# A ScalarE clock in the ordering model of a Trainium2 trunk kernel, and weight parts laid between a head's updates

## The chip, the core and the metric

The kernel runs on one core of a Trainium2 chip: TensorE (PE) multiplies, VectorE (DVE), ScalarE (ACT) and GpSimd (POOL) do the elementwise work, SyncE (SP) issues most transfers. Each engine takes its own instructions strictly in the order of the program and waits for others through semaphores. The metric is the device time of one execution in microseconds (us); less is better. The time before is the median of three runs.

## What is computed

A trunk of two layers on x of 1 x 1024 x 1024, all in float32. Layer 1 mixes tokens with a gated linear recurrence (8 heads of 128), layer 2 with attention in a window of 128; behind each stands a gated feed-forward part with a causal convolution of width 3. Every sublayer ends with a LayerNorm of ALPHA * h + sublayer. The change bears on the mixer of layer 1:

```python
def hgrn2_mixer(h, w_in, lower_bound, g_norm_w, w_out):
    q, f, i, g = jnp.split(h @ w_in, 4, axis=-1)
    ...
    fg = lb + (1.0 - lb) * jax.nn.sigmoid(heads(f))
    o = hgrn2_chunkwise(jax.nn.silu(heads(q)), 1.0 - fg, heads(i), jnp.log(fg))
    o = o * lax.rsqrt(jnp.mean(jnp.square(o), -1, keepdims=True) + RMS_EPS)
    o = o * g_norm_w * jax.nn.silu(heads(g))
    return o.reshape(B, S, D) @ w_out

# hgrn2_chunkwise, per head: S_t = diag(f_t) S_(t-1) + k_t v_t^T ;  o_t = S_t^T q_t
```

## The kernel before

A float32 product is made of three passes in a reduced format (`mm3`, L194 to L196): each operand is split into a high part, which ScalarE casts, and a low part, the rest, which VectorE subtracts (`low_part`, L169). L196 is the first pass that reads the low part of the weights.

The recurrence stage lies at some 24 to 545 us of the span. Its input products h @ w_in for heads 1 to 7 come in 14 units: unit 2(h-1) gives q and f of head h (kind "q"), the next one i and g (kind "v"). A unit is computed by a Strassen-Winograd scheme with seven products p1 to p7 of quarter matrices, each of 4 x 3 matmuls of 128x512, in the order 1, 5, 4 of the unit before, 6, 2, 3, 7. The weight side of a product is either a loaded quarter or a sum of quarters. `prepare` makes them: `cast` copies the high part on ScalarE (L1252, tile WR<-raw) and queues a job for the low part on VectorE (L169, WR<-raw,WR); sums of quarters are jobs too (L1260, raw<-raw,raw). WR has eight rows; `ROW` tells which product uses which. The four buffers raw0 to raw3 take the loaded quarters (L726, 512 KB each).

The results stand in four PSUM banks (psmm). `collect` has them read: ScalarE copies (L1320, L1334, L1388), VectorE additions (L1342, L1381, L1394) and gate functions (L1403, L1417, L1418, L1423).

Meanwhile the head before runs through `recur`: seven rounds of updates of qp, kp and tot on VectorE (`update`, L1095, L1097, L1100), scores on TensorE (L200, tile psax), masked placings of them on VectorE (`place`, L1038 and L1059), copies of halves on ScalarE (`stash`, L1082 and L1083) and of score blocks (L1076, L1154), transposes of the values (L204, VT to V, by L1388 and L1436), the products of values and keys (V,kd), a scan of the state St on VectorE (L1177, L1179), and the products V,A and St,qp that make the head's output.

The order in which all this is issued is set by `Order`, a small model that runs while the program is recorded. It carries a clock `t` for TensorE and `v` for VectorE; generators (`spawn`, `later`) are resumed when `t` reaches their due time, and between groups of matmuls `tick` lets them issue. Low parts and sums wait in the list `jobs`, first in, first out:

```python
def job(delay, us, make, key=None):
    jobs.append((od.t + delay, us, make, key))
def lay():
    if jobs and jobs[0][0] <= od.t:
        lay_job()
        return True
def need(key):
    while key not in done_jobs:
        lay_job()
```

`lay` is called as a filler when VectorE's clock is less than 1.5 us ahead; `product` calls `need`, which lays all jobs ahead of the one wanted. None of these times reach the chip; only the order does.

Ahead of the units, `sums_of` (L863) forms differences of quarters of the input on GpSimd, 12 subtractions of 128x512, read by ScalarE (L873) and VectorE (L874).

Of the kernel before, what the change touches and what calls it, by code (L numbers as in the profile page):

```python
# [54 lines left out]
class Order:  # L55
# [52 lines left out]
def trunk(ctx: ExitStack, tc: tile.TileContext, a: dict, out: bass.AP):  # L108
# [594 lines left out]
    with tc.tile_pool(name="t", bufs=1, reuse_waits="tile") as raws, hgrn_pool as hp:  # L703
# [29 lines left out]
        jobs, done_jobs = [], set()  # L733

        def job(delay, us, make, key=None):
            jobs.append((od.t + delay, us, make, key))

        def lay_job():
            ready, us, make, key = jobs.pop(0)
            make()  # L740
            od.vec(us)
            done_jobs.add(key)

        def lay():
            if jobs and jobs[0][0] <= od.t:
                lay_job()
                return True
            return False

        def need(key):  # L750
            while key not in done_jobs:
                lay_job()
# [107 lines left out]
        def sums_of(t):  # L860
            a11, a12, a21, a22 = [quarter(b, i) for b in (t, t + 4) for i in range(2)]
            for dst, x0, x1 in ((a11, a21, a11), (a21, a22, a21), (a22, a11, a22)):
                nc.gpsimd.tensor_tensor(dst, x0, x1, op=sub)  # L863

        def split_sum(t, which):
# [8 lines left out]
            job(0.9, 0.69, lambda: nc.vector.scalar_tensor_tensor(lo, src, scale, hi.bitcast(F32), op0=ALU.mult, op1=sub),  # L874
                ("x", which, t))

        with tc.tile_pool(name="ep", bufs=1, reuse_waits="tile") as ep:
# [33 lines left out]
            with tc.manual_schedule(engines={EN.PE, EN.SP, EN.Activation, EN.DVE}):  # L911
# [64 lines left out]
                for tp, after in ((2, 2), (1, 6)):  # L976
# [12 lines left out]
                for t in range(2, 4):  # L989
                    sums_of(t)  # L990
# [34 lines left out]
        def recur(h, qs, fg, kp):  # L1025
# [37 lines left out]
            def blocks(i, pv, K, Q):  # L1063
# [9 lines left out]
                def put():  # L1073
                    for b in range(P // (2 * m)):
                        o = 2 * m * b
                        nc.scalar.copy(A[o:o + m, :, o + m:o + 2 * m], pv[o:o + m, :, o + m:o + 2 * m])  # L1076
                return put

            def stash(i, t):
# [3 lines left out]
                nc.scalar.copy(halves(t)[:, :, 0, :], halves(kp)[:, :, 0, :])  # L1083
                return t
# [3 lines left out]
            def update(i):  # L1088
                m = 1 << i
                nb = S // (2 * m)  # L1090
                Tm, off = level
                qv = qp.rearrange("p (b u m) -> p b u m", u=2, m=m)
# [13 lines left out]
            nc.vector.tensor_tensor(r0, qs, kp, op=ALU.mult)  # L1106
            nc.vector.tensor_tensor(qp, qs, fg, op=ALU.mult)
            od.vec(4.4)
            r1 = hp.tile([P, S // 2], F32, name="r1")
            nc.vector.tensor_tensor(r1, kp[:, 0::2], qp[:, 1::2], op=ALU.mult)  # L1110
            update(0)
            gates_read[0] = h
            r2 = hp.tile([P, 2, S // 4, 2], F32, name="kd")
            for j in range(2):
                nc.vector.tensor_tensor(r2[:, j], kp[:, j::4].unsqueeze(2).to_broadcast([P, S // 4, 2]),
                                        qp.rearrange("p (b u) -> p b u", u=4)[:, :, 2:], op=ALU.mult)
            yield od.behind(-1.0, 5.0)
# [34 lines left out]
            for b in range(P // BL):  # L1152
                bs = slice(b * BL, (b + 1) * BL)
                nc.scalar.copy(A[bs, :, bs], Ab[bs])  # L1154
            yield wait
# [8 lines left out]
            nc.scalar.copy(kd, ps)  # L1164
            keys_done[0] = h
# [26 lines left out]
        def norm(h, pv):  # L1192
# [3 lines left out]
            for c in range(NB):  # L1196
                if c == NB // 2:
                    yield 2.4 if h < NH - 1 else 1.4
                nc.scalar.activation(junk, pv[:, c, :], AF.Square, accum_out=ss[:, c:c + 1])
            nc.gpsimd.tensor_scalar(ss, ss, 1.0 / P, RMS_EPS, op0=ALU.mult, op1=ALU.add)  # L1200
# [36 lines left out]
        last = len(units) - 1  # L1237
        raw_of, guard, ready, gated, turned = {}, [[] for _ in range(4)], [], {0}, set()
        ROW = {1: 0, 7: 1, 6: 2, 2: 3, 5: 4, 4: 5}
# [4 lines left out]
        def unit_load(u):  # L1244
            while u > 1 and ("lo", u - 2, 4) not in done_jobs:
                yield 0.2
            kind, h = units[u]
            raw_of[u] = [halves(column(g, h)) for g in ((0, 1) if kind == "q" else (2, 3))]

        def cast(u, p, src):  # L1250
            w = WR[0][:, row_of(u, p), :]
            nc.scalar.copy(w[:, :512], src)  # L1252
            job(0.8, 0.61, lambda: low_part(w[:, 512:], src, w[:, :512], None), ("lo", u, p))

        def prepare(u, stage):
# [4 lines left out]
            plus = lambda key, x, y: job(0.0, 0.61, lambda: tt(x, x, y, op=add), ("sum", u, key))  # L1260
            if stage == 0:
# [5 lines left out]
            elif stage == 2:  # L1267
                cast(u, 2, b21)
                plus(4, b21, b22)
            else:  # L1270
                prep[u, stage] = od.spawn(cast_sum(u, stage, *{5: (1, b11), 6: (2, b22), 7: (3, b12), 4: (4, b21)}[stage]))

        def cast_sum(u, p, after, src):
            while ("sum", u, after) not in done_jobs:
                yield 0.2
            yield max(od.v - od.t, 0.0)
            cast(u, p, src)

        def product(u, p):
            if (u, p) in prep:  # L1280
                drive(lambda: prep[u, p][1] is None)
            need(("lo", u, p))
# [12 lines left out]
        state, turning, prep = {}, [], {}  # L1295
# [14 lines left out]
        def keep_first(u, ps):  # L1310
# [9 lines left out]
            nc.scalar.copy((st["q"] if kind == "q" else VT)[:, :512], ps)  # L1320
            st["kept"] = True

        def keep(u, ps, cols):
# [10 lines left out]
            nc.scalar.copy(st["c"][:, cols], ps)  # L1334
            st[cols.start] = True

        def add_to(u, ps, cols, i):
# [5 lines left out]
            od.vec(0.61)  # L1343
            od.spawn(second(u, i), 0.8)
# [26 lines left out]
        def first(u, i, ps, n):  # L1371
            kind, h = units[u]
            st, ts = state[u], slice(i * 512, (i + 1) * 512)
            if i == 0:

                def sum11():
# [5 lines left out]
                    od.vec(0.61)  # L1382
                    if kind == "q":
                        od.spawn(first_query(u), 0.8)
                once(n, sum11())
                return
            if kind == "v":
                nc.scalar.copy(VT[:, ts], ps)  # L1388
                soon.append(od.spawn(turn_values(u), 0.9))
                return  # L1390
            nc.scalar.activation(st["q"][:, ts], ps, AF.Sigmoid)

            def query():
                tt(st["q"][:, ts], st["q"][:, ts], ps, op=ALU.mult)  # L1394
                od.vec(0.61)
                made(u)
            later(n, 1.0, query)

        def first_query(u):
# [4 lines left out]
            yield 0.8  # L1404
# [5 lines left out]
        def second(u, i):  # L1410
# [7 lines left out]
            nc.scalar.activation(fg[:, ts], fg[:, ts], AF.Identity, bias=lbt[:, 0, h:h + 1], scale=lbt[:, 1, h:h + 1])  # L1418
# [602 lines left out]
```

## Time and profile before

| | |
|---|---|
| median of three runs | 2170.17 us (2169.45 to 2171.3) |
| the profiled execution's own time | 2172.32 us |
| its span, first to last instruction | 2170.5 us |
| mean granted TensorE clock | 0.984 |
| PE, DVE, ACT, POOL busy | 2110.6, 1796.5, 971.3, 281.3 us |
| waits of TensorE for VectorE's low parts, 90 to 560 us | 26.2 us, 10 times |

A row of the timeline gives start and duration in us, engine, line, operation, the tile written and the tiles read, shapes, and how many instructions the row joins; in brackets stands how long the engine was idle before and what ended that. A row of stretches gives for each engine the busy time and the number of instructions, then the TensorE clock that was granted, where 1.00 is full speed. The profiled execution is one run; its time lies 2.15 us above the median of the three.

### The profile page before, as it was taken

The page shows a single profiled execution, that of the slowest core. Times are in us where ns is not written, and L with a number is a line of the kernel's source. Part 1 is how long each engine was busy: PE and PEld are TensorE (multiplying, and loading weights), DVE is VectorE, ACT ScalarE, POOL GpSimd, SP SyncE. Part 2 cuts the span into 40 slices and gives each one's busy share as a digit, 9 for nine tenths or more (in the row PEclk, how much of TensorE's full clock was granted, in tenths as well). Part 3 has the DMA queues.
Part 4 walks back from the last instruction along what each step waited for, and adds up shares of the span by engine and source line. Part 5 has one row for each costly group of instructions (what it writes and reads, how often), then busy time and mean ns, then how long its engine had stood idle before and what let it go on. Part 6 is the DMA issues. An engine that isn't in the chain of part 4 may idle for free.

```text
span 2170.5 us, 31768 instructions
## 1 busy us (share of the span) xinstructions
PE 2110.6 (97%) x12303; PEld 1757.1 (81%) x12303; DVE 1796.5 (83%) x2447; ACT 971.3 (45%) x1570; POOL 281.3 (13%) x307
## 2 busy tenths in 40 slices
PE   8798999989999999999999999999999999999998
PEld 7676878777888888888888888888888888888887
DVE  5756777776999999997887858979999999978986
ACT  5544555554254444444443256752444444444430
POOL 4000000100102111200000212331031112100002
PEclk9889999999999999999999999999999999999999
DMA  4101111133325557755965521133345587549762
GB/s 149 30 30 49 50 50 50 52 108 107 120 78 181 174 155 164 161 127 174 336 203 174 167 68 27 45 112 103 97 144 178 163 163 162 132 143 314 237 206 103
DMA packets 241271, 286.82 MB, mean 132 GB/s; under 512 B 30120, under 2 KB 160080, under 8 KB 241120
## 3 DMA queue, kind: packets, MB, share of 16 engines
q1 hardware_dynamic: 221600, 235.11, 33.5%
q0 software_dynamic: 19232, 49.54, 10.6%
q8 instruction: 97, 1.59, 0.3%
q14 instruction: 54, 0.44, 0.1%
q10 hardware_dynamic: 288, 0.14, 0.0%
HBM read 241.72 MB, written 89.15 MB: 152 GB/s over the span
## 4 chain that ended last, share of the span: by engine, by line
PE 89%; DVE 4%; ACT 2%; issue 2%; DMA 1%; POOL 1%; SPq 0%; DVEq 0%; POOLq 0%; ACTq 0%
PE psmm L196 18%; PE psmm L194 18%; PE psmm L195 18%; PE psax L194 9%; PE psax L196 9%; PE psax L195 9%; PE psax L200 3%; PE psmm L204 1%; PE psmm L200 1%; PE psax L1795 1%; PE psax L204 1%; DMA raw<-in_hgrn_w_in_dram 1%; DVE WR L169 1%; POOL XS L863 1%; PE psmm L1620 1%
## 5 line engine op out<-in xcount | busy, mean ns | idle before, releaser
L501 DVE SCALAR_TENSOR_TENSOR Y<-Y,cwt 128x1023 f32<-128x1023 f32 (+1 forms) x176 | 224.9, 1281 | 48.5 <-ACT Y L499 47.1
L221 ACT CAST HL<-rx 128x1024 fp32r<-128x1024 f32 (+1 forms) x151 | 150.6, 1006 | 155.8 <-PE psmm L195 24.7
L194 PE MATMUL psmm<-T,HL 128*128 128x512 f32 x512 | 200.7, 392 | 0.0
L196 PE MATMUL psmm<-T,HL 128*128 128x512 f32 x512 | 199.4, 390 | 0.0
L195 PE MATMUL psmm<-T,HL 128*128 128x512 f32 x512 | 199.4, 389 | 0.0
L169 DVE TENSOR_TENSOR HL<-rx,HL 128x1024 fp32r<-128x1024 f32 (+1 forms) x151 | 178.5, 1187 | 14.6 <-ACT HL L221 14.5
L499 ACT ACTIVATE Y<-Y,cwt 128x1024 f32<-128x1024 f32 x88 | 108.7, 1237 | 93.0 <-DVE Y L488 86.7
L243 POOL TENSOR_TENSOR rs<-rs,nhalf 128x1 f32<-128x1 f32 x32 | 45.3, 1415 | 725.2 <-DVE rs L242 725.2
L194 PE MATMUL psax<-T,HL 128*128 128x512 f32 x352 | 137.3, 390 | 0.0
L196 PE MATMUL psax<-T,HL 128*128 128x512 f32 x352 | 137.0, 389 | 0.0
L195 PE MATMUL psax<-T,HL 128*128 128x512 f32 x352 | 137.0, 389 | 0.0
L196 PEld LDWEIGHTS psmm<-T,HL 128*128 128x128 f32 x512 | 96.2, 188 | 20.2
L194 PEld LDWEIGHTS psmm<-T,HL 128*128 128x128 f32 x512 | 96.2, 188 | 19.5
L195 PEld LDWEIGHTS psmm<-T,HL 128*128 128x128 f32 x512 | 96.1, 188 | 19.5
L543 POOL COPY warm<-Y 128x1 f32<-128x1 f32 x64 | 63.9, 999 | 355.3 <-DVE Y L482 350.6
L194 PE MATMUL psmm<-T,WR 128*128 128x512 f32 x224 | 90.8, 405 | 7.8 <-ACT WR L1252 7.8
L196 PE MATMUL psmm<-T,WR 128*128 128x512 f32 x224 | 88.7, 396 | 5.9 <-DVE WR L169 5.9
L221 ACT CAST HT<-rx 128x1024 fp32r<-128x1024 f32 (+1 forms) x37 | 35.5, 959 | 129.7 <-DVE rx L456 62.4
L196 PE MATMUL psmm<-HL,WR 128*128 128x512 f32 x168 | 69.9, 416 | 22.8 <-DVE WR L169 22.8
L195 PE MATMUL psmm<-T,WR 128*128 128x512 f32 x224 | 88.4, 395 | 0.0
L1252 ACT CAST WR<-raw 128x512 fp32r<-128x512 f32 x98 | 58.7, 619 | 48.9 <-DMA raw<-in_hgrn_w_in_dram 35.1
L221 ACT CAST HL<-Y 128x1024 fp32r<-128x1024 f32 (+1 forms) x32 | 28.5, 892 | 115.8 <-DVE Y L456 40.9
(446 smaller groups left out, 6028.2 us busy)
## 6 DMA issues: line engine op xcount, KB each, us to landing
rx<-in_ffn_w_in_dram SPq DMA_DIRECT2D x136, 256.0 KB, 4.0
rx<-gd SPq DMA_DIRECT2D x118, 256.0 KB, 3.7
bsd<-in_ffn_w_out_dram POOLq DMA_DIRECT2D x36, 768.0 KB, 7.3
gd<-Y SPq DMA_DIRECT2D x44, 512.0 KB, 2.6
raw<-in_hgrn_w_in_dram SPq DMA_DIRECT2D x30, 512.0 KB, 5.0
rx<-in_ffn_w_out_dram SPq DMA_DIRECT2D x54, 256.0 KB, 4.3
R<-bsd SPq DMA_DIRECT2D x44, 256.0 KB, 5.1
Y<-in_ffn_w_in_dram SPq DMA_DIRECT2D x40, 256.0 KB, 4.2
```

Source lines behind the costliest of these rows:

```text
L169: make = lambda e: e.tensor_tensor(lo, src, hi.bitcast(F32), op=ALU.subtract)
L194: nc.tensor.matmul(ps, st(0), mv(0), start=start, stop=False, skip_group_check=more)
L195: nc.tensor.matmul(ps, st(0), mv(1), start=False, stop=False, skip_group_check=more)
L196: nc.tensor.matmul(ps, st(1), mv(0), start=False, stop=stop, skip_group_check=more)
L200: nc.tensor.matmul(ps, lhsT, rhs, start=start, stop=stop, **kw)
L204: nc.tensor.transpose(ps, src, ident)
L221: nc.scalar.copy(hi, src)
L243: nc.gpsimd.tensor_tensor(rs, rs, nhalf, op=ALU.pow)
L499: nc.scalar.activation(c, u, AF.Identity, bias=cwt[:, l, 3, ci:ci + 1], scale=cwt[:, l, 2, ci:ci + 1])
L501: nc.vector.scalar_tensor_tensor(c[:, sh:], u[:, :S - sh], cwt[:, l, 2 - sh, ci:ci + 1], c[:, sh:], op0=ALU.mult, op1=ALU.add)
L543: with tc.issue_after(nc.gpsimd.tensor_copy(tick, Y[:, 2 * (fc % 2) + (p == 4), :1]).ins):
L1252: nc.scalar.copy(w[:, :512], src)
```

## The change

What is computed stays, up to where six subtractions are done. The model gets a third clock, `a`, for ScalarE: `act` advances it where ScalarE's operations are recorded, and a low part is ready when the model's cast ends instead of at a fixed delay. TensorE's clock `t` moves forward where the model has it wait: in `need` to the time at which the job was laid, in `clear` to the time at which the bank is read. The list of jobs is no longer strictly first in, first out: jobs are grouped by unit (`group`), the first ready one of each group may go (`first_ready`), and `need` lays only jobs of its own group. `pressing` tells that a low part is needed within two products, or a sum within three, by `place_of`, the position of each product in the whole order; `breathe` lays one job of a unit that has a pressing one. It is called ahead of each placing and update and at three places in the first updates. Stages 0 and 2 of `prepare` become generators that wait for the modelled load (5 us) or for the stage before. The last six of the 12 subtractions of `sums_of` go from GpSimd to VectorE.

```diff
 class Order:
+        self.a = 0.0
+    def act(self, us, after=0.0):
+        self.a = max(self.a, self.t + 0.2, after) + us
+        return self.a
...
-        def lay_job():
-            ready, us, make, key = jobs.pop(0)
+        def lay_job(i=0):
+            ready, us, make, key = jobs.pop(i)
             make()
+            od.v = max(od.v, ready)
             od.vec(us)
             done_jobs.add(key)
+            laid_at[key] = od.v
+
+        def first_ready(due=lambda key: True):
+            seen = set()
+            for i, (ready, _, _, key) in enumerate(jobs):
+                if group(key) in seen:
+                    continue
+                seen.add(group(key))
+                if ready <= max(od.t, od.v) and due(key):
+                    return i
...
         def need(key):
             while key not in done_jobs:
-                lay_job()
+                lay_job(next(i for i, j in enumerate(jobs) if group(j[3]) == group(key)))
+            od.t = max(od.t, laid_at.get(key, 0.0))
+
+        def pressing(key):
+            if not key or key[0] not in ("sum", "lo"):
+                return False
+            p = key[2] if key[0] == "lo" else {1: 5, 2: 6, 3: 7, 4: 4}[key[2]]
+            return place_of[key[1], p] <= now[0] + (2 if key[0] == "lo" else 3)
+
+        def breathe():
+            i = first_ready(lambda key: any(pressing(j[3]) for j in jobs if group(j[3]) == group(key)))
+            if i is not None:
+                lay_job(i)
...
                 nc.vector.tensor_copy(msk, mf)
                 for t in range(2, 4):
-                    sums_of(t)
+                    sums_of(t, nc.vector)
...
             def place(dst, mi, src, view=lambda t: t):
                 mask = view(msk[:, mi * BL:(mi + 1) * BL])
+                breathe()
...
                 nc.scalar.copy(halves(t)[:, :, 0, :], halves(kp)[:, :, 0, :])
+                od.act(1.24, od.v)
...
-            job(0.8, 0.61, lambda: low_part(w[:, 512:], src, w[:, :512], None), ("lo", u, p))
+            job(od.act(0.6), 0.61, lambda: low_part(w[:, 512:], src, w[:, :512], None), ("lo", u, p))
...
         def clear(n):
             drive(lambda: all(t[1] is None for t in guard[n]))
             guard[n] = []
+            od.t = max(od.t, free_at[n])
...
-                while jobs and od.v < od.t + 1.5:
-                    lay_job()
+                while od.v < od.t + 1.5 and lay():
+                    pass
```

TensorE issues the same matmuls, VectorE six instructions more and GpSimd six fewer; SyncE's order stays. Three places show what moves. (In the changed kernel the lines have other numbers: L1303 is the cast of a high part, L174 the subtraction of a low part, L1311 a sum, L1131, L1133 and L1136 an update, L199 to L201 the three passes.)

*ScalarE, head 0, ahead of p5 of unit 1.* WR<-raw2 written by the single cast of raw2 is the high part for that product; kd is a stash, A the copies of score blocks. Before:

```order
L1320 COPY VT_107<-psmm_501 128x512
L1252 CAST WR_629<-raw0_99 128x512
L1252 CAST WR_629<-raw1_100 128x512
L1082 COPY kd_951<-qp_673 128x8x64
L1083 COPY kd_951<-kp_509 128x8x64
L1076 COPY A_117<-psax_899 32x8x32 x2
L1154 COPY A_117<-Ab_118 32x8x32 x4
L1252 CAST WR_629<-raw2_101 128x512
L1334 COPY GT_114<-psmm_502 128x512
```

After:

```order
L1303 CAST WR_629<-raw2_101 128x512
L1116 COPY kd_871<-qp_675 128x32x16
L1117 COPY kd_871<-kp_509 128x32x16
L1493 ACTIVATE fg_731<-fg_731 128x512
L1494 ACTIVATE fg_731<-fg_731,lbt_78 128x512
L1303 CAST WR_629<-raw3_102 128x512 x2
L1392 COPY VT_107<-psmm_501 128x512
L1303 CAST WR_629<-raw0_99 128x512
L1303 CAST WR_629<-raw1_100 128x512
L1407 COPY GT_114<-psmm_502 128x512
L1116 COPY kd_974<-qp_675 128x8x64
L1117 COPY kd_974<-kp_509 128x8x64
```

The cast of raw2 stood behind the stash and the copies into A and stands now ahead of an earlier stash; the read of p5's result (GT<-psmm_502) has come ahead of the later stash.

*VectorE, while head 2 runs, ahead of p6 of unit 4.* The low part for that product is WR<-raw1, the only one of raw1 in the first list and the first one in the second. Before:

```order
L1095 TENSOR_TENSOR qp_3645<-qp_3645,tot_3646 128x64x8
L1097 TENSOR_TENSOR kp_3536<-kp_3536,tot_3646 128x64x8
L1100 TENSOR_TENSOR tot_3646<-tot_3646 128x64
L1038 COPY_PREDICATED Ab_118<-msk_79,psax_3755 128x256
L1038 COPY_PREDICATED Ab_118<-msk_79,psax_3755 128x128
L1059 COPY_PREDICATED Ab_118<-msk_79,psax_3755 128x32x4
L1095 TENSOR_TENSOR qp_3645<-qp_3645,tot_3646 128x32x16
L1097 TENSOR_TENSOR kp_3536<-kp_3536,tot_3646 128x32x16
L1100 TENSOR_TENSOR tot_3646<-tot_3646 128x32
L1059 COPY_PREDICATED Ab_118<-msk_79,psax_3755 128x16x8
L1038 COPY_PREDICATED Ab_118<-msk_79,psax_3755 128x64x2 x2
L169 TENSOR_TENSOR WR_629<-raw1_100,WR_629 128x512
```

After:

```order
L1268 SCALAR_TENSOR_TENSOR GT_114<-psax_3732,par_76,GT_114 128x1024
L174 TENSOR_TENSOR WR_629<-raw1_100,WR_629 128x512
L1131 TENSOR_TENSOR qp_3649<-qp_3649,tot_3650 128x128x4
L1133 TENSOR_TENSOR kp_3518<-kp_3518,tot_3650 128x128x4
L1136 TENSOR_TENSOR tot_3650<-tot_3650 128x128
L174 TENSOR_TENSOR WR_629<-raw0_99,WR_629 128x512
L1311 TENSOR_TENSOR raw0_99<-raw0_99,raw1_100 128x512
L174 TENSOR_TENSOR WR_629<-raw1_100,WR_629 128x512
L1131 TENSOR_TENSOR qp_3649<-qp_3649,tot_3650 128x64x8
L1133 TENSOR_TENSOR kp_3518<-kp_3518,tot_3650 128x64x8
L1136 TENSOR_TENSOR tot_3650<-tot_3650 128x64
L1071 COPY_PREDICATED Ab_118<-msk_79,psax_3778 128x256
```

It stood behind the updates of 64- and 32-blocks and the placings of their scores, and stands now ahead of the update of 128-blocks.

*TensorE, p1 and p5 of unit 7.* psmm_501 takes p1, psmm_502 p5; V,A and St,qp make the output of the head that runs. Before (the end of the output's products, and what follows):

```order
L200 MATMUL psax_2542<-V_115,A_117 128x128
L200 MATMUL psax_2542<-St_2506,qp_2115 128x128
L194 MATMUL psmm_501<-T_81,WR_629 128x512
L195 MATMUL psmm_501<-T_81,WR_629 128x512
L196 MATMUL psmm_501<-T_81,WR_629 128x512
L194 MATMUL psmm_502<-T_81,WR_629 128x512
L195 MATMUL psmm_502<-T_81,WR_629 128x512
L196 MATMUL psmm_502<-T_81,WR_629 128x512
```

After (what precedes them, and their start):

```order
L199 MATMUL psmm_501<-T_81,WR_629 128x512
L200 MATMUL psmm_501<-T_81,WR_629 128x512
L201 MATMUL psmm_501<-T_81,WR_629 128x512
L199 MATMUL psmm_502<-T_81,WR_629 128x512
L200 MATMUL psmm_502<-T_81,WR_629 128x512
L201 MATMUL psmm_502<-T_81,WR_629 128x512
L205 MATMUL psax_2551<-V_115,A_117 128x128 x2
L205 MATMUL psax_2551<-St_2514,qp_2119 128x128
```

The output's products stood between the third and fourth group of p1, ahead of p5, and stand now behind the first group of p5. The scan of St on VectorE, which they read, stands ahead of p5's low part in both.

More of the change, by code (lines that the diff above doesn't have):

```diff
@@ L1164, in recur @@
             nc.scalar.copy(kd, ps)
+            od.act(1.0)
             keys_done[0] = h
@@ L1237, in trunk @@
         last = len(units) - 1
+        raw_at = {}
         raw_of, guard, ready, gated, turned = {}, [[] for _ in range(4)], [], {0}, set()
+        orders = {0: (1, 2, 5, 6, 3, 7), last - 1: (1, 5, 4, 6, 2, 7, 3), last: (1, 4, 6, 2, 7, 5, -4, 3)}
+        order_of = lambda u: orders.get(u, (1, 5, 4, 6, 2, 3, 7))
+        for u in range(last + 1):
+            for p in order_of(u):
+                place_of[(u - 1, 4) if p == 4 else (u, abs(p))] = len(place_of)
         ROW = {1: 0, 7: 1, 6: 2, 2: 3, 5: 4, 4: 5}
@@ L1259, in prepare, with begin @@
             (b11, b21), (b12, b22) = [(r[:, 0], r[:, 1]) for r in raw_of[u]]
-            plus = lambda key, x, y: job(0.0, 0.61, lambda: tt(x, x, y, op=add), ("sum", u, key))
-            if stage == 0:
+            plus = lambda key, x, y: job(od.t, 0.61, lambda: tt(x, x, y, op=add), ("sum", u, key))
+            def begin():
+                while od.t < raw_at[u]:
+                    yield 0.2
                 cast(u, 1, b11)
@@ L1266, in prepare, with middle @@
                 plus(2, b22, b11)
-            elif stage == 2:
+            def middle():
+                while prep[u, 1][1] is not None:
+                    yield 0.2
                 cast(u, 2, b21)
                 plus(4, b21, b22)
+            if stage == 0:
+                prep[u, 1] = prep[u, 3] = od.spawn(begin())
+            elif stage == 2:
+                prep[u, 2] = od.spawn(middle())
             else:
@@ L1281, in product @@
                 drive(lambda: prep[u, p][1] is None)
+            now[0] = place_of[u, p]
             need(("lo", u, p))
@@ L1293, in product, with read @@
             collect(u, p, ps)
-        state, turning, prep = {}, [], {}
+        state, turning, prep, free_at = {}, [], {}, [0.0] * 4
+        def read(n, us, vector=False):
+            if vector:
+                od.vec(us)
+                free_at[n] = od.v
+            else:
+                free_at[n] = od.act(us)
         def later(n, delay, make):
@@ L1320, in keep_first @@
             nc.scalar.copy((st["q"] if kind == "q" else VT)[:, :512], ps)
+            read(banks.index(ps), 0.6)
             st["kept"] = True
@@ L1334, in keep @@
             nc.scalar.copy(st["c"][:, cols], ps)
+            read(banks.index(ps), 0.6)
             st[cols.start] = True
@@ L1342, in add_to @@
             tt(st["c"][:, cols], st["c"][:, cols], ps, op=add)
-            od.vec(0.61)
-            od.spawn(second(u, i), 0.8)
+            read(banks.index(ps), 0.61, True)
+            od.spawn(second(u, i), max(od.v - od.t, 0.8))
         def collect(u, p, ps):
@@ L1388, in first @@
                 nc.scalar.copy(VT[:, ts], ps)
+                read(n, 0.6)
                 soon.append(od.spawn(turn_values(u), 0.9))
```

68 lines of the change are left out of this document (42 added, 26 removed).

## The prediction

> **What bounds the kernel now.** I read the page's busy line first, then busy time and clock by stretches, then the waits of TensorE, and for each long wait the queue of the engine that ended it.
>
> ```profile
> PE 2110.6 (97%) x12303; PEld 1757.1 (81%) x12303; DVE 1796.5 (83%) x2447; ACT 971.3 (45%) x1570; POOL 281.3 (13%) x307
> ```
>
> TensorE is busy 97% of the span, so the time can move only by idle time of TensorE and by stretches at a lower clock. The stretches below are cut where units of the recurrence stage begin; columns are length, busy time (and instructions) of PE, PEld, DVE, ACT and POOL, the granted clock, DMA share, GB/s.
>
> ```profile
> 24.00:73.25 49.25, 45.91 (x208) 37.65 (x207) 30.64 (x51) 29.78 (x54) 13.54 (x9) 0.90 0.08 22
> 73.25:138.49 65.24, 48.54 (x465) 38.54 (x464) 38.09 (x71) 25.09 (x56) 0.49 (x2) 0.82 0.12 33
> 138.49:202.31 63.82, 57.20 (x529) 47.98 (x528) 45.73 (x80) 29.48 (x62) 4.45 (x4) 0.95 0.08 26
> 202.31:420.03 217.72, 208.58 (x2066) 173.90 (x2064) 166.27 (x293) 114.67 (x245) 13.39 (x12) 0.98 0.16 50
> 259.18:310.63 51.45, 50.28 (x509) 41.81 (x508) 41.67 (x75) 29.03 (x62) 2.96 (x3) 1.00 0.17 52
> 420.03:473.44 53.41, 48.78 (x496) 40.16 (x495) 34.90 (x66) 25.73 (x56) 7.68 (x13) 0.94 0.21 62
> 473.44:513.60 40.16, 35.17 (x437) 27.95 (x436) 31.63 (x57) 21.58 (x34) 0.49 (x1) 0.96 0.45 149
> 545.00:2164.00 1619.00, 1617.82 (x7856) 1349.62 (x7854) 1413.36 (x1778) 698.95 (x1014) 227.98 (x247) 1.00 0.52 154
> ```
>
> From 545 us on, TensorE idles 1.2 us of 1619 at full clock: nothing can be won there, and the same matmuls are issued. The change is worth what it does between 24 and 514 us. The waits of TensorE in that stage, and the longest single ones (wait in brackets):
>
> ```profile
> PE psmm L196 <- DVE WR L169: 26.2, 10, 4.0
> PE psmm L194 <- ACT WR L1252: 8.2, 2, 7.8
> 105.67 0.79 PE L194 MATMUL psmm<-T,WR 128*128 128x512 f32 x1 [7.82 <-ACT WR L1252]
> 110.15 0.79 PE L196 MATMUL psmm<-T,WR 128*128 128x512 f32 x1 [3.26 <-DVE WR L169]
> 167.71 0.57 PE L196 MATMUL psmm<-HL,WR 128*128 128x512 f32 x1 [3.95 <-DVE WR L169]
> 181.32 0.53 PE L196 MATMUL psmm<-T,WR 128*128 128x512 f32 x1 [2.67 <-DVE WR L169]
> 217.92 0.50 PE L196 MATMUL psmm<-HL,WR 128*128 128x512 f32 x1 [3.38 <-DVE WR L169]
> ```
>
> Ten waits, 26.2 us, are for a low part of a weight piece (L169 on VectorE), two for its high part (L1252 on ScalarE). Neither engine is full; the piece stands behind other work. Three queues show it, in turn ScalarE ahead of 105.67, VectorE ahead of 167.71, VectorE ahead of 217.92:
>
> ```profile
> 101.56 0.62 ACT L1082 COPY kd<-qp 128x512 f32<-128x512 f32 x1
> 103.35 1.64 ACT L1154 COPY A<-Ab 32x256 f32<-32x256 f32 x4
> 105.00 0.62 ACT L1252 CAST WR<-raw 128x512 fp32r<-128x512 f32 x1
> 163.71 1.29 DVE L169 TENSOR_TENSOR WR<-raw,WR 128x512 fp32r<-128x512 f32 x2
> 166.97 0.69 DVE L169 TENSOR_TENSOR WR<-raw,WR 128x512 fp32r<-128x512 f32 x1
> 214.81 0.69 DVE L1095 TENSOR_TENSOR qp<-qp,tot 128x512 f32<-128x512 f32 x1 [1.72 <-ACT kd L1082]
> 217.16 0.71 DVE L169 TENSOR_TENSOR WR<-raw,WR 128x512 fp32r<-128x512 f32 x1
> ```
>
> The cast at 105.00 stands behind the copies of the running head. The low part that TensorE needs ends at 167.66, behind weight work of the next unit that was under way at 163.71. The one at 217.16 stands behind an update that itself waited 1.72 us.
>
> **The clock.** Three stretches of 3.41 us, each right behind a wait (3.95, 2.67 and 1.17 us):
>
> ```profile
> 284.20 0.50 PE L196 MATMUL psmm<-HL,WR 128*128 128x512 f32 x1 [1.17 <-DVE WR L169]
> 168.00:171.41 3.41, 3.41 (x40) 3.03 (x40) 0.86 (x2) 0.58 (x1) 0.00 (x0) 0.50 0.00 0
> 181.66:185.07 3.41, 3.41 (x18) 3.41 (x17) 0.81 (x2) 0.26 (x1) 0.00 (x0) 0.50 0.92 267
> 284.30:287.71 3.41, 3.41 (x22) 3.08 (x23) 1.09 (x4) 2.68 (x4) 0.00 (x0) 1.00 0.02 5
> ```
>
> So a wait of 2.67 us costs a further 3.41/2 = 1.7 us at half clock, one of 1.17 us none; I put the border between, near 2 us (estimate). [...]
>
> **Floors.** A product is 12 matmuls. Six start-to-start steps:
>
> ```profile
> 288.42 0.39 PE L195 MATMUL psmm<-T,WR 128*128 128x512 f32 x1
> 289.78 0.39 PE L195 MATMUL psmm<-T,WR 128*128 128x512 f32 x1
> ```
>
> 1.36/6 = 0.227 us, 2.72 us a product. The head from 259.18 has 14 products (38.1) in 50.28 us of busy time at full clock, so its recurrence takes 12.2 us of TensorE. Floors: 73.25 to 138.49 holds 11 products, 29.9 + 12.2 = 42.1; 138.49 to 202.31 holds 15, 53.0; the four heads from 202.31, 4 x 50.3 = 201.2.
>
> **The parts of the change, and their costs.** The clock for ScalarE, the waits that move the model's time, the release of jobs by unit and the pressing parts between updates go together: they add no work to a queue and give another order. I walked each queue in the new order by hand with the durations above.
>
> *First head, from 73.25.* The cast for its p5 now stands ahead of the copies, and low parts stand between updates; the idle time here, 65.24 - 48.54 = 16.7 us (11.1 of it in two waits quoted), loses its causes, and with it most of the half clock goes. By the walk one new wait appears, 1.7 us, where p4 waits for a bank that VectorE reads late; behind it on TensorE stand only further products. 42.1 + 1.7 = 43.8 against 65.24: gain 21.4. VectorE's 38.09 us of work would then fill 87% of the stretch, against 81% in the head at 259.18, and a walk sees each collision once; I take 2 off: 19.4. Ends: 10 (half of it) and 23.1 (floor).
>
> *Second head.* The needed low part is no longer behind the next unit; new waits of 1.5 and 0.95 us stay under the clock's border. 53.0 + 2.45 = 55.5 against 63.82: gain 8.3. Ends 3 and 10.8.
>
> *Four heads.* The part that ended at 217.87 now stands ahead of the scores, so this wait and its two like in later heads go. But p5's low part in a v unit now comes too late, because TensorE's products of state and scores, which stood ahead of p5, stand behind its third matmul. VectorE's queue there:
>
> ```profile
> 287.00 0.29 DVE L1177 COPY St<-psax 128x128 f32<-128x128 f32 x1 [2.25 <-PE psax L200]
> 287.32 2.27 DVE L1179 SCALAR_TENSOR_TENSOR St<-St,tot,psax 128x128 f32<-128x128 f32 x6
> 289.51 0.68 DVE L169 TENSOR_TENSOR WR<-raw,WR 128x512 fp32r<-128x512 f32 x1
> 290.11 0.68 DVE L1342 TENSOR_TENSOR fg<-fg,psmm 128x512 f32<-128x512 f32 x1
> ```
>
> The scan takes 2.5 us, each piece behind it 0.6 to 0.7. In u7, with five pieces: 2.5 + 4 x 0.6 + 0.7 = 5.6, against p1 and some of p5, 2.9: wait 2.7, clock 1.7; with 0.95 for the transpose of the values, 5.4. In u5 and u11 (scan and two pieces, 3.8, against three quarters of p1 and some of p5, 2.3) 1.5 each; in u9 the part stands ahead of the scan: none. Behind the waiting matmul stand the products of state and scores, for which ScalarE's squares wait; those have slack, as ScalarE's 114.67 us of 217.72 tell. 201.2 + 8.4 = 209.6 against 217.72: gain 8.1. Ends 0 (as many waits as before) and 16.5.
>
> *Last head, to 473.44.* Idle is 53.41 - 48.78 = 4.6, half clock up to 0.06 x 53.41 = 3.2: 7.8 at most; two new waits, 0.7 and 0.75, and some slack in the clock: gain 5. Ends 1 and 7.8.
>
> *Behind it, the values' transpose.* It is moved ahead of the sums and scores, but its copy on ScalarE still follows four casts that wait for loads.
>
> ```profile
> 484.21 1.05 ACT L1516 CAST HL<-raw 128x1024 fp32r<-128x1024 f32 x1 [0.20 <-DMA raw<-in_hgrn_w_out_dram]
> 488.72 1.02 PE L204 MATMUL psax<-ident,VT 128*128 128x128 f32 x4 [3.08 <-ACT VT L1388]
> ```
>
> The last cast ends at 485.26; two moves of 1.05 and a copy put the transpose 1 us earlier, but 3.4 us of scores that filled the time stand behind it now: wait 5.6 in place of 3.08. Loss 2.5, and half a microsecond for a low part of the output weights: 3. Ends: loss 6, gain 3.
>
> *Six subtractions from GpSimd to VectorE.* ScalarE waited for GpSimd three times:
>
> ```profile
> 42.37 0.63 ACT L873 ACTIVATE HL<-XS 128x512 fp32r<-128x512 f32 x1 [2.64 <-POOL XS L863]
> 45.49 0.63 ACT L873 ACTIVATE HL<-XS 128x512 fp32r<-128x512 f32 x1 [0.30 <-POOL XS L863]
> 49.39 0.63 ACT L873 ACTIVATE HL<-XS 128x512 fp32r<-128x512 f32 x1 [3.27 <-POOL XS L863]
> 71.36 0.69 DVE L1562 TENSOR_TENSOR qs<-qs,psmm 128x512 f32<-128x512 f32 x1
> ```
>
> Those 6.2 us go, but six pieces of 0.61 (3.7) join the queue ahead of the multiplication at 71.36, which frees a bank for the second product; the walk gives 1.0 more for the low parts ahead of it: gain 1.5. Ends -3.7 and 6.2.
>
> The order of loads on SP stays; the loads of the convolution's parameters shift under idle queues, at nothing; if uncovered, their casts cost some tenths.
>
> Sum: 19.4 + 8.3 + 8.1 + 5 - 3 + 1.5 = 39.3. The profiled execution took 2172.32, which gives 2133.0; the median is 2.15 lower, 2130.9.
>
> **Rivals.** (a) *Nearly all waits go* (0.16): the new ones are my walk's errors. Then 23.1 + 10.8 + 16.5 + 7.8 = 58, 2112. For it: no engine but TensorE is full. Against: VectorE is in order and at 81% even in the best head.
>
> (b) *New waits take the old ones' place* (0.22): each of 14 units gets one of some 1.5 us and half of them a half clock, 21 + 12 = 33 of 58 given back: gain 25 down to 10, 2145 to 2160. For it: the scan and the ScalarE copies still stand in order ahead of parts. Against: the waits of 7.82, 3.95 and 3.38 us each have one cause in a queue, and it is gone.
>
> (c) *Slower* (0.08): ScalarE's cast of a freshly loaded piece stands in order ahead of the stash copies that a head's updates need. If a load came so late that it held ScalarE a whole transfer (5.14 us in the row below), each of seven heads would lose 5.1 and 1.7 of clock, 48 in all: 2179. It decides above 39.3/7 = 5.6 us a head. Against: casts waited for loads already, and ScalarE has 45% of work.
>
> ```profile
> 316.85 5.14 DMA raw<-in_hgrn_w_in_dram
> ```
>
> (d) *It doesn't do what it says* (0.04): other queues end the same waits, and the time stays within 0.2% (4.3 us, about what a measurement of this kernel can tell from no change).
>
> **Chances and range.** The forecast, 2122 to 2142, has 0.5. The range takes in most of (a) and of (b): 2114 to 2157; some 0.2 is left out. Faster: 0.5 + 0.16 + 0.22, less 0.01 for the far end of (b) = 0.87; same 0.05; slower 0.08.
>
> **What would show it.** Right: from the first head's second product to its last (65.24 now) some 44 to 46 us at a clock of 0.95 or more; the wait for L1252 gone; four heads at about 52 each, p5 of some v units waiting 1.5 to 2.7; the values' transpose of the last head waiting over 4 us. Wrong: the first head above 52 us, waits of over 2 us in each head, or ScalarE waiting for DMA ahead of stash copies.

## The result, and the profile after

The changed kernel takes 2138.12 us (median of four runs, 2136.97 to 2139.92) against 2170.74 for the one before (four runs, 2169.45 to 2171.65): 32.6 us less, ratio 0.9851, 95% interval 0.9834 to 0.9868. Its profiled execution took 2138.2 us with a span of 2136.4, 34.1 less than before.

The busy line of the page after:

```profile
PE 2095.7 (98%) x12303; PEld 1747.3 (82%) x12303; DVE 1797.0 (84%) x2453; ACT 971.0 (45%) x1570; POOL 271.7 (13%) x301
```

The same matmuls take 14.9 us less of busy time, and the mean granted clock rose from 0.984 to 0.994: TensorE spent less time at half clock. The stretches of the changed kernel, cut at the same matmuls as before (columns as there):

```profile
24.00:72.81 48.81, 43.41 (x211) 35.90 (x211) 34.06 (x59) 31.52 (x59) 4.33 (x3) 0.96 0.08 23
72.81:116.52 43.71, 42.67 (x464) 35.26 (x465) 35.64 (x67) 20.38 (x37) 0.00 (x0) 0.97 0.17 49
116.52:172.38 55.86, 54.12 (x531) 45.05 (x530) 46.51 (x80) 32.50 (x78) 6.29 (x5) 1.00 0.16 48
172.38:384.25 211.87, 206.09 (x2065) 172.19 (x2064) 165.56 (x293) 114.75 (x244) 11.99 (x16) 0.99 0.17 51
384.25:437.19 52.94, 49.16 (x497) 40.56 (x496) 36.51 (x70) 25.73 (x55) 6.64 (x9) 0.94 0.13 41
437.19:477.94 40.75, 33.22 (x422) 26.35 (x421) 27.45 (x49) 21.88 (x34) 0.58 (x1) 0.96 0.42 147
```

The first head went from 65.24 to 43.71 us, with TensorE busy for 42.67 of them. The second gained 8.0, the four heads 5.9, the last 0.5. From there to the same point among the last output's products 38.6 us became 40.75: 477.94 us here, 512.1 before, where the prediction's row ends 1.5 us later, at 513.6. In the long stretch behind the recurrence nothing moved: TensorE is busy for 1617.7 of 1619 us from 511 us on, against 1617.8 from 545 us on before.

The four largest groups of waits of TensorE from 24 to 560 us, and then single waits in the stage, with the instructions of VectorE that ended two of them (scan and low part ahead of 259.96, copy of the parameters ahead of 401.03):

```profile
PE psax L209 <- ACT VT L1462: 5.7, 2, 5.2
PE psmm L201 <- DVE WR L174: 5.5, 4, 2.6
PE psmm L199 <- DVE qs L1641: 4.2, 1, 4.2
PE psax L209 <- DVE cwt L1039: 3.6, 1, 3.6
72.81 0.79 PE L199 MATMUL psmm<-T,WR 128*128 128x512 f32 x1 [4.17 <-DVE qs L1641]
123.77 0.47 PE L199 MATMUL psmm<-T,WR 128*128 128x512 f32 x1 [1.51 <-DVE GT L1416]
205.46 0.50 PE L201 MATMUL psmm<-T,WR 128*128 128x512 f32 x1 [1.34 <-DVE WR L174]
254.51 2.27 DVE L1222 SCALAR_TENSOR_TENSOR St<-St,tot,psax 128x128 f32<-128x128 f32 x6
259.22 1.89 DVE L174 TENSOR_TENSOR WR<-raw,WR 128x512 fp32r<-128x512 f32 x3
259.96 0.66 PE L201 MATMUL psmm<-T,WR 128*128 128x512 f32 x1 [2.58 <-DVE WR L174]
364.88 0.50 PE L201 MATMUL psmm<-T,WR 128*128 128x512 f32 x1 [1.34 <-DVE WR L174]
400.69 0.27 DVE L1039 COPY cwt<-psax 128x88 f32<-128x88 f32 x1
401.03 1.94 PE L209 MATMUL psax<-ident,VT 128*128 128x128 f32 x8 [3.57 <-DVE cwt L1039]
451.47 1.12 PE L209 MATMUL psax<-ident,VT 128*128 128x128 f32 x4 [5.22 <-ACT VT L1462]
```

From 24 to 560 us low parts held TensorE up for 28.7 us in eleven waits before (the 26.2 us in ten are those from 90 us on); now for 5.5 in four, and the wait of 7.82 for a cast is gone. What is left are mostly new waits: for the multiplication that frees the bank of unit 0's second product (L1641), for the parameters' copy, and for p5's low part in three v units. The wait for the copy of the last values is an old one that grew, from 3.08 to 5.22 us.

### The profile page after: what moved, and what is told of

Same layout as the page of the kernel before. It is cut to its first block, busy times and chain, and to the rows that moved or that the text cites. A ratio compares the mean times of both kernels' runs of the same rounds, so it can differ in the third digit from the quotient of the medians.

```text
span 2136.4 us, 31777 instructions
## 1 busy us (share of the span) xinstructions
PE 2095.7 (98%) x12303; PEld 1747.3 (82%) x12303; DVE 1797.0 (84%) x2453; ACT 971.0 (45%) x1570; POOL 271.7 (13%) x301
## 3 DMA queue, kind: packets, MB, share of 16 engines
q1 hardware_dynamic: 221600, 235.11, 34.1%
## 4 chain that ended last, share of the span: by engine, by line
PE 93%; DVE 3%; DMA 1%; ACT 1%; issue 1%; POOL 0%; SPq 0%; DVEq 0%; ACTq 0%; POOLq 0%
PE psmm L199 18%; PE psmm L201 18%; PE psmm L200 18%; PE psax L199 9%; PE psax L201 9%; PE psax L200 9%; PE psax L205 4%; PE psmm L209 1%; PE psmm L205 1%; PE psax L209 1%; PE psax L1873 1%; PE psmm L1698 1%; DMA raw<-in_hgrn_w_in_dram 1%; DVE WR L174 0%; DMA raw<-in_hgrn_w_out_dram 0%
## 5 line engine op out<-in xcount | busy, mean ns | idle before, releaser
L199 PE MATMUL psmm<-T,HL 128*128 128x512 f32 x512 | 200.6, 392 | 0.0
L201 PE MATMUL psmm<-T,HL 128*128 128x512 f32 x512 | 199.4, 389 | 0.0
L174 DVE TENSOR_TENSOR HL<-rx,HL 128x1024 fp32r<-128x1024 f32 (+1 forms) x151 | 178.4, 1187 | 15.8 <-ACT HL L226 15.6
L199 PE MATMUL psax<-T,HL 128*128 128x512 f32 x352 | 137.3, 390 | 0.0
L201 PE MATMUL psax<-T,HL 128*128 128x512 f32 x352 | 137.0, 389 | 0.0
L201 PEld LDWEIGHTS psmm<-T,HL 128*128 128x128 f32 x512 | 96.2, 188 | 20.1
L199 PEld LDWEIGHTS psmm<-T,HL 128*128 128x128 f32 x512 | 96.1, 188 | 19.6
L199 PE MATMUL psmm<-T,WR 128*128 128x512 f32 x224 | 91.5, 409 | 6.7 <-DVE qs L1641 4.2
L201 PE MATMUL psmm<-T,WR 128*128 128x512 f32 x224 | 88.8, 397 | 5.3 <-DVE WR L174 5.3
L174 DVE TENSOR_TENSOR WR<-raw,WR 128x512 fp32r<-128x512 f32 x98 | 63.9, 685 | 21.0 <-ACT WR L1303 21.0
L201 PEld LDWEIGHTS psax<-T,HL 128*128 128x128 f32 x352 | 66.0, 188 | 13.8
```

The lines of the kernel that those rows point to most:

```text
L174: make = lambda e: e.tensor_tensor(lo, src, hi.bitcast(F32), op=ALU.subtract)
L199: nc.tensor.matmul(ps, st(0), mv(0), start=start, stop=False, skip_group_check=more)
L201: nc.tensor.matmul(ps, st(1), mv(0), start=False, stop=stop, skip_group_check=more)
```

## The experiments

Twelve kernels were run, each beside the kernel before. The table has the length in us of the stretches, cut at the same matmuls in each trace (unit 0's second product, unit 1's last, first products of units 4 and 12, p5 of the last unit; each at its start), then span and median time.

| kernel | to first cut | first head | second | four heads | last | rest | span | median |
|---|---|---|---|---|---|---|---|---|
| before | 73.3 | 65.2 | 63.8 | 217.7 | 53.4 | 1697.1 | 2170.5 | 2170.7 |
| changed | 72.8 | 43.7 | 55.9 | 211.9 | 52.9 | 1699.2 | 2136.4 | 2138.1 |
| e1, no pressing | 71.3 | 50.2 | 61.0 | 205.9 | 51.2 | 1694.4 | 2134.0 | 2138.0 |
| e2, sums on GpSimd | 72.4 | 42.3 | 55.9 | 211.7 | 52.8 | 1699.2 | 2134.1 | 2136.0 |
| e3, t without waits | 72.3 | 43.1 | 69.5 | 217.0 | 51.5 | 1694.1 | 2147.4 | 2151.7 |
| e4, no ScalarE clock | 72.2 | 49.4 | 56.3 | 204.8 | 50.3 | 1690.6 | 2123.6 | 2125.9 |
| e5, waits alone | 71.4 | 50.8 | 60.3 | 204.8 | 53.5 | 1689.7 | 2130.5 | 2132.7 |
| e6, pressing alone | 71.4 | 46.7 | 67.0 | 213.5 | 48.2 | 1690.4 | 2137.1 | 2140.6 |
| e7, ScalarE clock alone | 72.2 | 53.5 | 74.8 | 239.3 | 50.3 | 1697.5 | 2187.4 | 2186.7 |
| e8, none of the three | 71.8 | 52.5 | 66.2 | 215.3 | 48.2 | 1690.3 | 2144.3 | 2146.2 |
| e9, none, prepared at once | 71.7 | 51.7 | 66.3 | 204.2 | 49.5 | 1690.1 | 2133.5 | 2136.5 |
| e10, ScalarE clock early | 72.3 | 42.3 | 57.7 | 204.8 | 49.6 | 1690.4 | 2117.1 | 2117.3 |
| e11, parameters and tail | 71.5 | 43.8 | 55.9 | 212.0 | 47.3 | 1695.5 | 2126.0 | 2128.2 |
| e12, before with one rule | 71.4 | 50.6 | 69.2 | 206.9 | 50.0 | 1694.2 | 2142.4 | 2144.2 |

The 95% interval of each ratio reaches some 0.15% to each side, about 3 us. So a difference of less than about 5 us between two of these kernels is not clear of noise by the times alone; the traces have to carry it.

**One part taken away.** First each of the model's parts was taken out of the changed kernel by itself, and the subtractions were put back.

```diff
 # e1
         def breathe():
+            return
 # e2
-                    sums_of(t, nc.vector)
+                    sums_of(t, nc.gpsimd)
 # e3, in need and in clear
-            od.t = max(od.t, laid_at.get(key, 0.0))
-            od.t = max(od.t, free_at[n])
 # e4
-        self.a = max(self.a, self.t + 0.2, after) + us
+        self.a = self.t + 0.2 + us
```

> The changed kernel, but no part is laid between a head's updates: breathe returns at once. Theory A (the pressing parts are what takes low parts out from behind updates and placings): the waits of TensorE for low parts come back, about 3.4 us with 1.7 us of half clock every second head and as much in the first head, 12 to 18 us in all, some 2150 to 2156 us. Theory B (the model's clocks alone, by putting the head's groups later among the products, did it): within 4 us of the changed kernel's 2138.

> The changed kernel with its last six subtractions back on GpSimd. The rest of the order is the same on TensorE. Theory A (by the trace the move gained only 0.4 us up to unit 0's second product, since the multiplication that frees its bank now stands behind the six): within 2 us of 2138, the second product again at 72 to 74 us. Rival (the move is worth what ScalarE waited for GpSimd, 6.2 us, and the wait of 4.2 us has another cause): 4 to 6 us slower. A second rival (the queue on VectorE is the whole of that wait): 2 to 4 us faster.

> The changed kernel, but the model's clock of TensorE doesn't move with waits (neither in need nor in clear). Theory A (the pressing parts carry the gain, the clock's moves only refine it): 3 to 8 us slower, 2141 to 2146. Theory B (the clock that moves with waits is what puts a head's groups where their inputs are ready): 12 to 25 us slower, with new waits of TensorE for placings and updates.

> The changed kernel, but ScalarE's clock carries nothing over: each operation ends 0.2 us and its own length after TensorE's clock, as with fixed delays. Theory A: the read of the bank of unit 1's p5 stands again behind a stash and six copies in the first head, one wait of 2 to 4 us there, 3 to 8 us slower in all. Theory B (the model's clocks did it): 10 us slower or more, spread over all heads.

Without pressing parts: 2138.01, ratio to before 0.9847 (0.9832 to 0.9861), no different in total. The table tells why: the first two heads lose 6.5 and 5.1 us, and the stretches behind win as much. The total is theory B's; theory A's waits come back, but only in the first two heads:

```profile
97.93 0.80 PE L201 MATMUL psmm<-T,WR 128*128 128x512 f32 x1 [3.55 <-DVE WR L174]
160.45 0.80 PE L201 MATMUL psmm<-T,WR 128*128 128x512 f32 x1 [4.06 <-DVE WR L174]
```

In the four heads there is now no wait of half a microsecond at all. So the pressing parts, together with the ScalarE clock (without which these waits are gone too, below), made the waits of 1.34 and 2.58 us.

With the subtractions on GpSimd: 2136.00, 0.9835 (0.9819 to 0.9851). The second product starts 0.4 us earlier, its wait of 4.17 us and the half clock behind it are gone, and the first head takes 42.3 in place of 43.7. So the move costs some 2 us, 1.9 of them in these two stretches, though the intervals of the two kernels overlap. The time is that of the second rival, its cause is not. The first product of unit 0 on TensorE and the multiplication on VectorE, in the changed kernel and then in e2:

```profile
65.76 0.39 PE L199 MATMUL psmm<-T,WR 128*128 128x512 f32 x1
72.07 0.68 DVE L1641 TENSOR_TENSOR qs<-qs,psmm 128x512 f32<-128x512 f32 x1
69.65 0.39 PE L199 MATMUL psmm<-T,WR 128*128 128x512 f32 x1
71.63 0.68 DVE L1641 TENSOR_TENSOR qs<-qs,psmm 128x512 f32<-128x512 f32 x1
```

With the subtractions on VectorE TensorE comes 3.9 us earlier to this place, but the multiplication is no earlier: 71.36 us before the change, 72.07 with it, 71.63 in e2. In the changed kernel the six subtractions end at 54.67. What stands right ahead of the multiplication are the low parts and sums of unit 0, from 64.47 on, with 1.9 us in which VectorE waits for ScalarE's casts. The time won turns into one wait of 4.17 us, and half clock lies on its end and behind it, from 72.41 to 75.82 us.

Without the moves of TensorE's clock: 2151.73, 0.991 (0.9895 to 0.9925), 13.6 us slower than the changed kernel, as theory B said. The loss is in the second and third head, the first has none. The waits are not those that theory B named: from the second head to the end of the four heads they are for low parts (6.6 us, five times), for a cast (3.9) and for banks (4.3); one of 3.1, ahead of a head's scores, has no cause in the profile.

Without ScalarE's clock: 2125.86, 0.9793 (0.9778 to 0.9807), 12.3 us faster, which neither theory had. By the table the first head loses 5.7 us; the four heads win 7.1, the last 2.6, the rest 8.6. In the first head p5 of unit 1 waits again, 1.7 us for its cast and 2.9 for its low part; the wait for a bank that theory A named is not seen. The new waits that the prediction had priced in the four heads and in the last values' transpose are gone there. Its three longest groups of waits from 172 to 560 us are:

```profile
PE psmm L199 <- DVE Y L359: 2.9, 1, 2.9
PE psmm L199 <- ACT fg L1407: 1.8, 1, 1.8
PE psax L209 <- ACT VT L1462: 0.6, 2, 0.3
```

**One part alone.** Then each part by itself, and none, by the same edits together.

> Of the change's three parts in the model only the moves of TensorE's clock with waits are left; no pressing parts, no carried ScalarE clock. If the parts add up (theory C: without pressing 0 us, without ScalarE's clock 12.3 us faster, both measured one by one), 2138 - 0.1 - 12.3 = 2126. Rival D (they stand in for each other: without pressing the first two heads lost 6.5 and 5.2 us, without ScalarE's clock the first head lost 5.7): both losses together in the first two heads and no gain in later ones beyond one of them, 2130 to 2136.

> Only the pressing parts are left; TensorE's clock doesn't move with waits and ScalarE's carries nothing over. Theory C: 2138 + 13.6 - 12.3 = 2139. Rival D: 2143 or more.

> Only ScalarE's clock is left. Theory C: 2138 - 0.1 + 13.6 = 2152. Rival D (a clock of ScalarE that TensorE's clock doesn't follow puts copies where they are late): 2156 or more.

> None of the three parts; what is left is the queue by unit, the weight preparation as tasks that wait for the modelled load, no forced laying of jobs, and the subtractions on VectorE. Theory C: 2138 - 0.1 + 13.6 - 12.3 = 2139, so that most of the change's gain over 2171 would come from this rest. Rival D: 2155 to 2171, the gain comes from the three parts.

Measured: 2132.72 (0.9824, 0.9808 to 0.9841), 2140.59 (0.9861, 0.9846 to 0.9876), 2186.68 (1.0072, 1.0056 to 1.0087) and 2146.22 (0.9886, 0.9872 to 0.9901). The parts don't add up: rival D's figures hold for the first and the third, the second lies nearer to theory C's 2139, and the last is between the two. Without all three, 24.5 of the 32.6 us remain. Set beside each other, in us:

| | without ScalarE's clock | with it |
|---|---|---|
| neither of the others | 2146.2 | 2186.7 |
| pressing | 2140.6 | 2151.7 |
| moves with waits | 2132.7 | 2138.0 |
| both | 2125.9 | 2138.1 |

The moves with waits win in each pair (13.5 and 14.7 without the clock, 48.7 and 13.6 with it). Pressing wins 5.6 and 6.9 without the clock, 35 beside the clock alone, nothing in total beside clock and moves. ScalarE's clock loses in each row: 40.5, 11.1, 5.3, 12.3; the 5.3 and 5.6 are hardly clear of noise. Alone it gives twelve waits for low parts and four for casts:

```profile
PE psmm L201 <- DVE WR L174: 30.4, 12, 5.4
PE psmm L199 <- ACT WR L1303: 12.7, 4, 6.1
```

A likely reason, argued and not shown: in a model whose TensorE doesn't wait, ScalarE falls ever further behind, the low parts come due too late, and are laid too late.

**The rest.** What makes the 24.5 us? With jobs laid by force again in the kernel of e8, every engine's rows keep their order, so this edit can't. With all jobs in one group the changed kernel keeps its order too. The kernel of e8 does not: parts of its order on VectorE, ScalarE and TensorE become another, and that was not timed, so what the release by unit gives there stays open. The next experiment undid the waiting tasks of the preparation, the one after it put the rule by which a job counts as ready into the kernel before:

```diff
 # e9, on top of e8's edits
             if stage == 0:
-                prep[u, 1] = prep[u, 3] = od.spawn(begin())
+                cast(u, 1, b11)
+                cast(u, 3, b22)
+                plus(1, b11, b12)
+                plus(3, b12, b22)
+                plus(2, b22, b11)
             elif stage == 2:
-                prep[u, 2] = od.spawn(middle())
+                cast(u, 2, b21)
+                plus(4, b21, b22)
 # e12, in the kernel before
-            if jobs and jobs[0][0] <= od.t:
+            if jobs and jobs[0][0] <= max(od.t, od.v):
```

> The kernel without the three parts (2146), and in addition the first and third stage of the weight preparation issue their casts and sums at once, as before the change, instead of waiting as tasks for the modelled load. What is left of the change are VectorE's shares in the model and the subtractions on VectorE. Theory E (a cast of a piece that is still being loaded blocks ScalarE's queue in the first heads, and waiting for the modelled load was the larger part of the 24.5 us between 2171 and 2146): 2160 to 2172. Rival F (the order changed because VectorE's work is counted otherwise in the model): 2142 to 2152.

> The kernel before with one line changed: a waiting job may be laid if its due time is not past the later of TensorE's and VectorE's clock in the model, where before it had to be past TensorE's. In the model VectorE's clock runs ahead of TensorE's whenever VectorE has work, and then this fills a place that would be left to updates. Theory I (this rule is what is left of the change when its three parts and the waiting tasks are taken away, and it makes most of that kernel's gain): 2130 to 2145, the first head 50 to 53 us, the second 64 to 68. Rival J (the gain of that kernel needs the other ways in which it counts VectorE's work): 2158 to 2171.

With the preparation at once 2136.48 (0.9844, 0.9827 to 0.9861): faster than e8 by 9.7 us, so both theories miss, E on the wrong side; the third head alone wins 11 (the four heads 215.3 to 204.2). Waiting for the modelled load costs here, where the three parts are missing. The one rule in the kernel before gives 2144.20 (0.9885, 0.9869 to 0.9902), 25 us of the change's 32.6, as theory I said, though the second head, 69.2, is longer than it gave and than before. The rule does not make all of e9, the kernel that it was to explain: e12 is 7.7 us slower, most of it in the second head, the four heads and the rest. The longest wait of each of its first three heads:

```profile
95.83 0.80 PE L196 MATMUL psmm<-T,WR 128*128 128x512 f32 x1 [4.77 <-DVE WR L169]
165.06 0.80 PE L194 MATMUL psmm<-T,WR 128*128 128x512 f32 x1 [3.41 <-ACT WR L1252]
206.38 0.50 PE L196 MATMUL psmm<-HL,WR 128*128 128x512 f32 x1 [2.96 <-DVE WR L169]
```

Behind the third of these there is no wait of 1 us up to the last head. VectorE's clock in the model runs ahead of TensorE's while VectorE has work; a job due by then is laid under the new rule and left standing under the old. How much of the rule's gain is in the changed kernel's own 32.6 us once the three parts are there was not tried.

**Two places, and a better kernel.** The last two were built from these readings.

```diff
 # e11
-            yield 330.0
+            yield 300.0
...
-                        if p in (7, 5):
-                            for k in range(2):
-                                out_split(k + (2 if p == 5 else 0))
+                        if p == 4:
+                            for k in range(4):
+                                out_split(k)
 # e10, with e2's edit; od.late is 1e9 until the 14th product of the order, then od.t
-        self.a = max(self.a, self.t + 0.2, after) + us
+        self.a = max(self.a if self.t < self.late else 0.0, self.t + 0.2, after) + us
```

> The changed kernel with two places moved: the convolution's parameters 30 us earlier in the model, so that their transposes stand behind a head's last transpose and not ahead of the transpose of the values, and the casts of the output weights behind the copy of the last values. Theory (two waits, 3.57 us with half clock and 5.22 us with half clock, have these two causes): the last head 52.9 to 48 to 50 us, the stretch behind it 40.75 to 35 to 37 us, 2128 to 2132 in all. Rival (other work ends the same waits): each stretch within 1 us of the changed kernel's, 2136 to 2139.

> The changed kernel with ScalarE's clock carried only up to the second head's first products, and the six subtractions back on GpSimd. Theory G (each stretch depends on the model's state there alone, so that stretches of different runs can be put together): from unit 0's second product 42 to 45 us as with the clock, the four heads 205 and the last one 50 as without it, sum 2116 to 2120. Rival H (the first head leaves another phase to the heads behind it, and the stretches don't add): 2124 to 2138.

With both places moved 2128.15 (0.9808, 0.979 to 0.9826). The last head takes 47.3 in place of 52.9, without the wait for the parameters' copy (3.57 us) and the 6.83 us at half clock on it and behind it, so these had cost some 5.6; the stretch to the last output's products takes 37.3 in place of 40.75, just outside the 35 to 37 that were expected, because the output weights' low parts, cast later, now hold TensorE up:

```profile
448.71 0.80 PE L1698 MATMUL psmm<-HL,T 128*128 128x512 f32 x1 [4.66 <-DVE HL L174]
```

With ScalarE's clock in the first head only, 2117.34 (0.9757, 0.974 to 0.9773): theory G. The first head, the four heads and the last one came as put together, and it is some 21 us faster than the changed kernel; only the second head, 57.7, is longer than in either parent (55.9 in e2, 56.3 in e4). Its longest groups of waits from 72 to 560 us:

```profile
PE psmm L200 <- DVE Y L360: 2.9, 1, 2.9
PE psmm L200 <- ACT fg L1410: 1.8, 1, 1.8
PE psmm L202 <- DVE WR L175: 1.6, 1, 1.6
```

## Why the prediction was right, and where not

The direction and the range held: 2138.1 in 2114 to 2157, 7 above the forecast of 2131 and within its inner band of 2122 to 2142. The signs named beforehand came: the wait for a cast (L1252) gone, four heads at 53.0 on the mean, p5 of three v units waiting 1.34 to 2.58, the values' transpose 5.22; the first head was even a little shorter than the 44 to 46. By its terms, from the stretches:

- *First head, 19.4 forecast:* 21.5 measured. The 2 us that I took off for VectorE's load were wrong: at 82% VectorE (35.64 of 43.71) was no further limit. That the walk's own length, 43.8, was met (43.71) is in part luck. The one wait that it priced at 1.7 was 1.04; the half clock that runs on to 75.82 us from the wait at 72.81, 1.5 us, was in no term; and e2, with the same wait and full clock, takes 42.3, so the floor is 41.2 and not 42.1.
- *Second head, 8.3:* 8.0. The wait for a bank, priced 1.5, measured 1.51. The other, priced 0.95, did not come (1.74 us idle in all), but TensorE's busy time at full clock, 54.1, is 1.1 above the floor of 53.0: two misses that partly cancel.
- *Four heads, 8.1:* 5.9. The new waits came where the walk put them, at nearly their sizes: u5 and u11 1.34 each (1.5), u7 2.58 with a half clock (2.7), the values' transpose 0.52 (0.95). The floor was mis-sized: the head from 280.95 has no idle time and takes 50.85, not 50.3, and the four heads of e4, which wait 0.6 us in all, take 204.8 and not 201.2.
- *Last head, 5:* 0.5, the largest miss. I had let the parameters' loads shift at nothing, and the two waits of this stretch stood in the sum at 0.7 and 0.75. One wait alone, for the parameters' copy, was 3.57, and half clock lay on it and behind it, from 400.09 to 406.91. The copy (400.69) stands behind updates and placings on VectorE, and the values' transpose waits for it. e11 gives 5.6 for it.
- *Values' transpose, loss of 3:* 2.1. The wait was 5.22 (5.6 forecast), and the casts ahead of its copy were its cause; e11 shows that without them the low parts of the same weights are next, 4.66 us.
- *Subtractions, gain of 1.5:* 0.4 to the first cut, and a half clock behind it, so that e2 without the move is 2 us faster. The sign was wrong. The step that failed is to take ScalarE's 6.2 us, less what joins VectorE's queue, as won at the second product: e2 shows that TensorE did come 3.9 us earlier, but that the multiplication, which stands behind the low parts and sums of unit 0, did not, and that the wait for it brought a half clock that had no price in the sum.

Sum: 39.3 forecast against 34.1 in the spans and 32.6 in the medians.

Most queues were read rightly, but what the prediction took for the cause of the new order was wrong in part. I had put the clock for ScalarE, the moves with waits, the release by unit and the pressing parts down as working together. Of these the clock for ScalarE costs 12.3 us, the release by unit changes nothing in the changed kernel's order, and the pressing parts give nothing in total once the other two are there. The rule on ready jobs, which makes 25 us alone in the kernel before, the prediction didn't mention. A walk through the final order can price a change without telling which of its lines did it.

Of the rivals, (b) was partly so: new waits took some 7.5 us of the four heads (1.34 twice, 2.58 with 1.7 of clock, 0.52) and more at the end. (a), (c) and (d) did not come. No wait that (c) describes is among those of TensorE.

## What to carry to other kernels

When an ordering model is improved in several ways at once, undo each way by itself and try each alone: a truer clock for one engine made the order worse, and one small rule, put alone into the kernel before, gave 25 us where the whole change gave 32.6. Price the order by walking the queues with measured durations, place by place, and give the rare side jobs (parameters, last casts) the same care as the loop, since the misses were there. Where stretches between fixed matmuls behave alike in several variants, the best of each can be put together: that gave 2117 in the one case tried.

## What was not expected of the hardware

The prediction put a border near 2 us: a longer wait of TensorE would cost it half its clock for 3.41 us, a shorter one nothing. For the one wait to which it was applied this held (2.58 us at 259.96 in the changed kernel, with half clock from 260.14 to 263.55), and behind the waits of 1.34 us at 364.88 and of 1.51 us at 123.77 there was none. In other kernels it failed. Behind the third wait of e12, 2.96 us at 206.38, the clock stayed at 1.00, and so it did behind 3.60 us in e1, but behind 1.84 us in e10 it was 0.50. The granted clock behind the waits at 364.88 and 259.96 (changed kernel), at 206.38 (e12), at 454.75 (e1) and at 398.67 (e10), with the rows of the last two:

```profile
365.00:368.41 3.41, 3.41 (x30) 3.36 (x31) 3.38 (x6) 0.64 (x2) 0.00 (x0) 1.00 0.00 0
260.14:263.55 3.41, 3.41 (x16) 3.31 (x16) 3.38 (x6) 0.72 (x1) 0.00 (x0) 0.50 0.00 0
206.38:209.79 3.41, 3.41 (x90) 2.78 (x92) 0.00 (x0) 1.31 (x2) 0.00 (x0) 1.00 0.00 0
454.75 0.66 PE L209 MATMUL psax<-ident,VT 128*128 128x128 f32 x4 [3.60 <-ACT VT L1463]
454.75:458.16 3.41, 3.41 (x20) 2.62 (x24) 2.81 (x7) 2.97 (x6) 0.00 (x0) 1.00 0.01 2
398.67 0.50 PE L200 MATMUL psmm<-HL,WR 128*128 128x512 f32 x1 [1.84 <-ACT fg L1410]
399.99:403.40 3.41, 3.41 (x39) 2.78 (x38) 1.04 (x2) 0.58 (x1) 0.00 (x0) 0.50 0.00 0
```

So these rows show no border: full clock stood behind 2.96 and 3.60 us, half clock behind 1.84 and 2.58. What decides between the two is not shown. In the changed kernel's trace half clock ran from 72.41 to 75.82, from 260.14 to 263.55, from 400.09 to 406.91 and from 451.29 to 454.70 us, on or right behind the waits of 4.17, 2.58, 3.57 and 5.22 us, and not behind those of 1.34 and 1.51. Here, then, a single wait of 1.84 to 3.60 us was followed by 3.41 us at half clock, a loss of 1.7 us, in some places and by full clock in others, and a difference of that size between two of the kernels above is by itself no sign of a better order.
